# A two-layer encoder on one core: the MLP products on pairs of 2-byte floats, with range sums and the former program behind a branch

## The chip, the cores and the metric

One core of a Trainium2 chip (trn2) runs the whole forward pass as one program. The metric is the device time of one execution in microseconds (us). Engines are named as in the profile: PE multiplies matrices (PEld is its weight load), DVE, ACT and POOL work on vectors, SP issues most of the DMAs.

## The reference, cut to what matters

Two layers on a sequence of 1024 rows of width 1024. Each layer has a token mixer (latent attention in layer 0, dilated windows in layer 1) and then an MLP with a hidden width of 4096. All tensors are float32. What the change touches is the last two lines:

```python
for i in range(DEPTH):                       # 2
    ...
    x = x + gate1 * y                        # y: the token mixer
    h = rms_norm(x, norm_mlp[i]) * (1 + scale2) + shift2
    x = x + gate2 * (jnp.square(jax.nn.relu(h @ mlp_w1[i])) @ mlp_w2[i])
```

## The kernel before

**How a product is made.** PE multiplies in a reduced float32 form (`fp32r`). A float32 factor x is therefore split in two: ACT copies it to the high part (`split`, line 121, or `form`, line 375), DVE subtracts to get the low part (line 122, or line 376). A product is three matmuls, high by high, high by low and low by high (`mm3`, lines 425 to 427). In the MLPs each of them has 128x128 weights and 512 moving columns.

**Both MLPs** (`mlp7`) cut each of the two big products into 2 x 2 blocks and use seven block products where eight would be plain. The block sums that this needs are made on DVE (line 1098, the helper `tt`) before the split.

The *up* half goes over 16 chunks `c` of 256 hidden columns and seven products each: 12 matmuls per product (4 blocks of depth, 3 matmuls). For each chunk DVE makes four weight sums (`ws`), seven low parts (`wf`), seven reads of PSUM (`ua`, `u`, `ub`) and four sums of results (`us`, `ua`); ACT makes seven high parts, relu and square (lines 1139, 1140). POOL stores the seven result blocks to DRAM (`uf`). A form is written in the code four products ahead of its use.

The *down* half goes over seven products and eight groups `g`, 24 matmuls per step. A step loads a block of `uf` and a block of `mlp_w2` (`d_load`, tiles `ufr` and `w2r`), and splits both (`d_form`, tiles `dh` and `dl`). For the first of the seven products each group loads two blocks of `mlp_w2` into the pool `G` and subtracts one from the other (`w2r<-w2r,w2r`, 1024 columns); the later products reuse them.

At the start of the up half two things overlap: the last matmuls of the mixer's output projection (`psy`), and the making of seven forms of h (`h_forms`, tiles `hk`, `hs`, `ht`, `hf`), each in two tiles of 1024 columns. The first six chunks have their first weights formed early (`mlp_early`, tiles `w1h`, `wf` in the pool `G`), so that PE starts with 12 products that need only two of the seven forms of h.

**What sets the order.** The framework places each engine's instructions by a timeline of its own while it builds the program, so that a load or a vector operation stands where its buffers are expected to be free, often far from where the code calls it. Each engine then runs its queue in order. The buffers of `G` (29, also for `hf`, early `wf`, `woh`, `oT`, `w2r` of the first down product) and of `X` (20, for `w1r`, `ws`, other `wf`, `ufr`, `dh`, `dl`) are 4 KB per partition each, whatever a tile uses of it.

**The branch that is there already.** `bias_check` (line 1366 on) finds on the chip whether the positions are evenly spaced; the flag is read by every engine (line 1396) and a branch (line 1484) skips the general bias tables.

Of the kernel before, what the change touches and what calls it, by code (L numbers as in the profile page):

```python
# [20 lines left out]
P = 128  # L21
D = 1024
# [19 lines left out]
class K:  # L42
    def __init__(self, ctx, tc, a, ng=29):
        self.ctx, self.tc, self.nc, self.a = ctx, tc, tc.nc, a
        nc = tc.nc
        self.cp = ctx.enter_context(tc.tile_pool(name="const", bufs=1))
# [5 lines left out]
        self.n = 0  # L52
        self.ax = None
# [16 lines left out]
    def nm(self, s):  # L70
        self.n += 1
        return f"{s}_{self.n}"
# [10 lines left out]
    def C(self, name, shape, dt=F32):  # L83
        return self.cp.tile(list(shape), dt, tag=name, name=name)

    def M(self, name, shape, dt=F32):
        return self.mp.tile(list(shape), dt, tag=name, name=name)


    def setup(self):  # L90
# [5 lines left out]
        nc.vector.memset(self.ones, 1.0)  # L96
        self.mods = {}
        self.gates = self.dp.tile([4, 1024], F32, name="gates")
        self.onerow = self.dp.tile([1, S], F32, name="onerow")
# [19 lines left out]
    def split(self, hi, lo, src, lo_eng=None):  # L119
        nc = self.nc  # L120
        nc.scalar.activation(hi, src, AF.Copy)  # L121
        (lo_eng or nc.vector).tensor_tensor(lo, src, hi.bitcast(F32), op=ALU.subtract)  # L122
# [31 lines left out]
    def consts(self, psp):  # L154
# [6 lines left out]
        self.pinned(nc.vector.tensor_copy(self.colc, ps[:, 0:136]))  # L161

# [54 lines left out]
    def ada_col(self, l, s, c, n, ps):  # L217
# [7 lines left out]
        nc.vector.tensor_tensor(mo, ps, self.colc[:, b : b + nd], op=ALU.add)  # L225
# [9 lines left out]
    def ada_end(self, l, s, acc, row, psp, tag):  # L235
# [3 lines left out]
        if s % 3 == 2:  # L239
            for h in range(2):  # L240
                ps, c = PS(), slice(h * 512, (h + 1) * 512)
                nc.tensor.matmul(ps[0:1, :], self.ones[:, 0:1], acc[:, c], start=True, stop=True)
                nc.vector.tensor_tensor(row[0:1, c], ps[0:1, :], row[0:1, c], op=ALU.add)
# [118 lines left out]
    def h_forms(self, xs0, xs1, mods, xalloc):  # L362
# [176 lines left out]
    def mla(self, xs, ada0, xs1, mods, tail):  # L539
# [168 lines left out]
        qkv = self.dp.tile([H, S, 256], F32, name="qkv")  # L708
        hw = [w0, []]
        heads, maxes = {}, {}  # L710
        md, ld, rd = (self.dp.tile([H, S], F32, name=x) for x in ("mrow", "lrow", "rrow"))
# [126 lines left out]
        oTd = self.dp.tile([4, 2, P, 2, 512], F32, name="moTd")  # L838
# [170 lines left out]
    def proj_res(self, O, order, wo, gate, xs, mods, xalloc, done, more, first=None):  # L1009
# [4 lines left out]
        with self.tc.tile_pool(name="psO", bufs=2 if first else 6, space=PSUM, reuse_waits="tile") as psp:  # L1014
# [21 lines left out]
            pss = []  # L1036
            (at, steps), (at1, steps1) = self.h_forms(xs[0:4], xs[4:8], mods, xalloc)
# [29 lines left out]
    def w1_form(self, src, alloc):  # L1067

        g = alloc("wf", (P, 2, 4, P))
        self.split(g[:, 0], g[:, 1], src)  # L1070
        return g

    def mlp_early(self, l, E):
# [7 lines left out]
        def form(c):  # L1081
            raw = raws.pop(c)
            for g in range(2):
                Ls[c][f"L1{g + 1}"] = self.w1_form(raw[:, 4 * g : 4 * g + 4, :], self.G)
# [3 lines left out]
    def mlp7(self, l, early, R, steps, xd, out, more=(), nxt=None, keep=None):  # L1088
# [10 lines left out]
        uf = self.dp.tile([7, NP, P, 512], F32, name=f"uf{l}")  # L1099
# [5 lines left out]
        with self.tc.tile_pool(name="psM", bufs=8, space=PSUM, reuse_waits="tile") as psp:  # L1105
# [23 lines left out]
            def up(u, i):  # L1129
# [6 lines left out]
                def square(o, x, y):  # L1136
# [3 lines left out]
                    nc.scalar.activation(o, o, AF.Square)  # L1140
# [46 lines left out]
            def d_form(i, g, ld):  # L1187
# [8 lines left out]
                split(u)  # L1196
                if rn == "R11":
                    split(q["11"])
                if rn == "R11":
# [129 lines left out]
            for n, (i, gr) in enumerate(dsteps):  # L1329
# [20 lines left out]
                if n == last - 1:  # L1350
                    continue
                for t in range(4):
# [13 lines left out]
    def bias_check(self, psp):  # L1366
# [5 lines left out]
        self.bias = [self.dp.tile([9, H, self.HS], F32, name=f"bias{g}") for g in range(3)]  # L1372
# [10 lines left out]
        nc.vector.tensor_scalar(fl, ps[0:1, 0:1], 0.0, None, op0=ALU.is_equal)  # L1383

        pf = self.G("posrf", (8, P), F32)
# [5 lines left out]
        self.fl = fl  # L1391

    def bias_even_load(self):

        nc = self.nc
        loads, (self.even,) = nc.values_load_multi_w_load_instructions(
# [1024 lines left out]
```

## Time and profile before

| what | us |
|---|---|
| runs, lowest / median / highest of 3 | 3220.20 / 3229.61 / 3231.48 |
| profiled execution, first to last instruction (span) | 3228.3 |
| what lies around the span (median of the runs less the span; the profiled execution's own time is not given apart) | 1.3 |
| MLP of layer 0, first to last matmul, about | 777 to 1402 |
| MLP of layer 1, first to last matmul, about | 2602 to 3222 |
| PE busy / DVE busy / ACT busy | 3127.8 / 2381.4 / 1734.1 |

In the profile a matmul's own duration is longer than the distance to the next one, since matmuls are pipelined: what counts for the time is the distance from start to start. A row of the timeline has the start in us, the duration in us, engine, line, operation, output tile and input tiles, shapes and count. A row of the windows has, for a stretch of the span, its length and each engine's busy time with the number of instructions in brackets, then the granted clock of PE (1.00 is full speed), the DMA engines' busy share and GB/s. In the list of groups the two numbers behind the bar are busy us and mean ns of one instruction.

### The profile page before, as it was taken

How to read it: one execution, taken by the hardware profiler on the slowest of the kernel's cores; microseconds unless marked ns; L12 is line 12 of the kernel's file. 1: busy time of each engine (PE TensorE's matmuls, PEld its weight loads, DVE VectorE, ACT ScalarE, POOL GpSimd, SP SyncE). 2: the span in 40 equal slices, each digit the busy share in tenths (PEclk: the TensorE clock that was granted, in tenths of full speed). 3: DMA queues.
4: the chain of work that ended last, by engine and by line, in shares of the span. 5: the costliest groups of instructions: out<-in, count | busy, mean ns of one | idle time of the engine just before them, and what ended most of it. 6: DMA issues, size and time to landing. Idle time of an engine off the chain costs nothing. (4 is left out here: it accounts for less than half of the span.)

```text
span 3228.3 us, 50796 instructions
## 1 busy us (share of the span) xinstructions
PE 3127.8 (97%) x18034; PEld 2646.1 (82%) x18034; DVE 2381.4 (74%) x4243; ACT 1734.1 (54%) x3507; POOL 919.3 (28%) x1226
## 2 busy tenths in 40 slices
PE   6989999999999999989999999998999999999999
PEld 6877677778788788877889998998998888888887
DVE  5677777746977776688857777777887588778566
ACT  5547777754544443542226777667665264544342
POOL 6464556530111100001123435444454001110010
PEclk8999999999999999999999999999999999999999
DMA  5352322253554779555648777887777536448554
GB/s 193 121 190 79 106 87 92 67 170 111 181 200 170 270 218 315 171 194 172 213 128 185 180 174 177 185 196 169 173 159 199 171 105 214 150 151 313 202 190 130
DMA packets 540014, 554.41 MB, mean 172 GB/s; under 512 B 199493, under 2 KB 421106, under 8 KB 539754
## 3 DMA queue, kind: packets, MB, share of 16 engines
q1 hardware_dynamic: 501962, 445.10, 48.7%
q0 software_dynamic: 27360, 91.31, 7.6%
q10 hardware_dynamic: 10432, 14.68, 1.6%
q8 instruction: 144, 2.36, 0.3%
q14 instruction: 116, 0.95, 0.1%
HBM read 378.27 MB, written 132.62 MB: 158 GB/s over the span
## 5 line engine op out<-in xcount | busy, mean ns | idle before, releaser
L426 PE MATMUL psm<-dl,dh 128*128 128x512 f32 x896 | 351.1, 392 | 8.6 <-DVE dl L122 8.4
L425 PE MATMUL psm<-hf,wf 128*128 128x512 f32 x896 | 350.2, 391 | 2.6 <-ACT wf L121 2.6
L427 PE MATMUL psm<-dh,dl 128*128 128x512 f32 x896 | 350.2, 391 | 0.0
L426 PE MATMUL psm<-hf,wf 128*128 128x512 f32 x896 | 349.4, 390 | 0.0
L427 PE MATMUL psm<-hf,wf 128*128 128x512 f32 x896 | 346.9, 390 | 0.4 <-DVE wf L122 0.4
L425 PE MATMUL psm<-dh,dh 128*128 128x512 f32 x896 | 334.7, 391 | 4.7 <-ACT dh L121 4.7
L425 PE MATMUL psproj<-wqkh,hTp 128*128 128x256 f32 x1024 | 302.7, 296 | 0.0
L427 PE MATMUL psproj<-wqkh,hTp 128*128 128x256 f32 x1024 | 291.5, 285 | 0.0
L426 PE MATMUL psproj<-wqkl,hTp 128*128 128x256 f32 x1024 | 291.3, 285 | 0.0
L121 ACT ACTIVATE dh<-ufr 128x1024 fp32r<-128x1024 f32 x112 | 118.4, 1057 | 173.1 <-PE psm L427 50.1
L426 PEld LDWEIGHTS psm<-dl,dh 128*128 128x128 f32 x896 | 169.0, 189 | 46.7 <-DVE dl L122 11.8
L425 PEld LDWEIGHTS psproj<-wqkh,hTp 128*128 128x128 f32 x1024 | 197.6, 193 | 8.4 <-issue 0.2
L425 PEld LDWEIGHTS psm<-dh,dh 128*128 128x128 f32 x896 | 168.4, 188 | 41.8 <-ACT dh L121 6.8
L425 PEld LDWEIGHTS psm<-hf,wf 128*128 128x128 f32 x896 | 168.7, 188 | 40.2 <-ACT wf L121 5.5
L427 PEld LDWEIGHTS psm<-hf,wf 128*128 128x128 f32 x896 | 168.5, 188 | 36.0 <-DVE wf L122 1.2
L426 PEld LDWEIGHTS psproj<-wqkl,hTp 128*128 128x128 f32 x1024 | 197.8, 193 | 0.2 <-DVE wqkl L122 0.2
L427 PEld LDWEIGHTS psproj<-wqkh,hTp 128*128 128x128 f32 x1024 | 197.6, 193 | 0.2
L427 PEld LDWEIGHTS psm<-dh,dl 128*128 128x128 f32 x896 | 169.0, 189 | 34.8
L426 PEld LDWEIGHTS psm<-hf,wf 128*128 128x128 f32 x896 | 168.7, 188 | 34.6
L122 DVE TENSOR_TENSOR dl<-ufr,dh 128x1024 fp32r<-128x1024 f32 x112 | 136.9, 1222 | 77.8 <-ACT dh L121 59.1
L756 DVE TENSOR_REDUCE mx<-pmx 128x1 f32<-128x512 f32 x256 | 165.0, 682 | 27.6 <-PE pmx L754 27.4
L122 POOL TENSOR_TENSOR pl<-p,ph 128x1024 fp32r<-128x1024 f32 x58 | 141.3, 2435 | 136.2 <-ACT ph L121 125.9
(400 smaller groups left out, 8917.1 us busy)
## 6 DMA issues: line engine op xcount, KB each, us to landing
ufr<-uf SPq DMA_DIRECT2D x112, 512.0 KB
adaw<-in_ada_w SPq DMA_DIRECT2D x96, 512.0 KB
w2r<-in_mlp_w SPq DMA_DIRECT2D x96, 512.0 KB
w1r<-in_mlp_w SPq DMA_DIRECT2D x64, 512.0 KB
bt<-bias SPq DMA_DIRECT2D x128, 256.0 KB
wqkr<-in_dil_w_in SPq DMA_DIRECT2D x96, 256.0 KB
wvr<-in_dil_w_in SPq DMA_DIRECT2D x34, 512.0 KB
qkv<-st SPq DMA_DIRECT2D x32, 512.0 KB
```

What stands on the lines that cost most here:

```text
L121: nc.scalar.activation(hi, src, AF.Copy)
L122: (lo_eng or nc.vector).tensor_tensor(lo, src, hi.bitcast(F32), op=ALU.subtract)
L425: mm(out, lh, rh, start=first, stop=False)
L426: mm(out, lh, rl, start=False, stop=False)
L427: mm(out, ll, rh, start=False, stop=last)
L756: nc.vector.tensor_reduce(maxes[h][:, 2 * j + b : 2 * j + b + 1], ps, op=ALU.max, axis=AX.X)
```

## The change

- **2-byte pairs in the MLPs.** All operands of both MLPs' matmuls (`hf`, `wf`, and `d` for the former `dh`, `dl`) become pairs of float16 in one tile of 4 KB (`pair`), where two tiles of 4 KB or one tile of two float32 halves stood. The number of matmuls, their shapes and the three-matmul scheme stay. PE gets a separate weight load for each matmul. The mixers stay as they are.
- **Scales.** Powers of two keep the values in the range of float16: h is 16 times as large (folded into the modulation's rows), weights 512 times (in the copy and the subtraction), the square takes a scale of 2^-10, the gate 2^-15.
- **Range sums.** The low part is made by one DVE instruction that scales, subtracts and also sums the low part over the columns into a column of a tile `seen` (`parts`). Three high parts per layer are summed in absolute value (`floor`). At the end of each MLP these columns are folded to one number per partition, and at the very end of the second one a comparison and a 1x1 matmul give one flag (`verdict`, `verdict_sum`).
- **The former program behind a branch.** `program` calls `run` twice: once as described, and once more, with the float32 forms and tiles named `r_...`, inside `tc.If(k.good_value == 0)`. Every engine reads the flag and branches at its end. The bias tables are shared.

The core of the diff:

```diff
+    def pair(self, alloc, name, shape):
+        if self.half:
+            g = alloc(name, (shape[0], 2) + tuple(shape[1:]), F16)
+            return g[:, 0], g[:, 1]
+        return tuple(alloc(name + k, shape) for k in "hl")
...
+    def parts(self, hi, lo, src, scale=1.0):
+        if not self.half:
+            return self.split(hi, lo, src)
+        nc = self.nc
+        nc.scalar.activation(hi, src, AF.Copy, scale=scale)
+        self.nseen += 1
+        return nc.vector.scalar_tensor_tensor(lo, src, scale, hi, op0=ALU.mult, op1=ALU.subtract,
+                                              accum_out=self.seen[:, self.nseen - 1 : self.nseen])
...
+    def fold(self, k):
+        tr, s = self.nc.vector.tensor_reduce, self.seen
+        tr(self.bad[:, k : k + 1], s[:, 0 : self.nseen], op=ALU.add, axis=AX.X, apply_absolute_value=True)
+        tr(self.bad[:, k + 2 : k + 3], s[:, 509 : self.nlow + 1], op=ALU.min, axis=AX.X)
...
+        nc.vector.tensor_scalar(t[:, 0:2], self.bad[:, 0:2], 512.0, None, op0=ALU.is_le)
+        nc.vector.tensor_scalar(t[:, 2:4], self.bad[:, 2:4], 128.0, None, op0=ALU.is_ge)
+        nc.vector.tensor_reduce(m, t, op=ALU.min, axis=AX.X)
...
+        nc.tensor.matmul(ps[0:1, 0:1], m, self.ones[:, 0:1], start=True, stop=True)
+        self.good = self.C("good", [1, 1], I32)
+        nc.vector.tensor_scalar(self.good, ps[0:1, 0:1], float(P), None, op0=ALU.is_equal)
...
-            g = [self.G("hf", (P, 2, 512)) for _ in range(2)]
-            nc.scalar.activation(g[0], src, AF.Copy)
-            lo = nc.vector.tensor_tensor(g[1], src, g[0].bitcast(F32), op=ALU.subtract)
+            g = self.pair(self.G, "hf", (P, 2, 512))
+            lo = self.parts(*g, src)
...
-        g = alloc("wf", (P, 2, 4, P))
-        self.split(g[:, 0], g[:, 1], src)
+        g = alloc("wf", (P, 2, 4, P), F16 if self.half else F32R)
+        self.parts(g[:, 0], g[:, 1], src, self.ws)
...
-                def split(x):
-                    r.extend(self.X("d" + k, (P, 2, 512)) for k in "hl")
-                    self.split(*r[-2:], x)
+                def split(x, scale=self.ws):
+                    r.extend(self.pair(self.X, "d", (P, 2, 512)))
+                    self.parts(*r[-2:], x, scale)
...
 def program(tc, a):
+    with tc.tile_pool(name="shared", bufs=1, space=DRAM) as shared:
+        k = run(tc, a, True, shared)
+        with tc.If(k.good_value == 0):
+            run(tc, a, False, shared, k)
```

With the buffers that the pairs leave free, the framework orders some queues anew. Three places matter. First PE, at the first product of layer 0's MLP (`hf` are the forms of h, `wf` the formed weights). Before:

```order
L425 MATMUL psm_14029<-hf_13717,wf_13875 128x512
L426 MATMUL psm_14029<-hf_13718,wf_13875 128x512
L427 MATMUL psm_14029<-hf_13717,wf_13875 128x512
L425 MATMUL psm_14029<-hf_13717,wf_13875 128x512
L426 MATMUL psm_14029<-hf_13718,wf_13875 128x512
```

And now:

```order
L504 LDWEIGHTS wf_13879
L504 MATMUL psm_14034<-hf_13724,wf_13879 128x512
L505 LDWEIGHTS wf_13879
L505 MATMUL psm_14034<-hf_13724,wf_13879 128x512
L506 LDWEIGHTS wf_13879
L506 MATMUL psm_14034<-hf_13724,wf_13879 128x512
```

The weight load is an instruction of its own, and both halves of a form of h lie in one tile. The matmuls are the same.

Second SP's queue, at the start of the same MLP (`w1h` and `w1r` are raw weights of the up half, `w2r` those of the down half). Before:

```order
L431 DMA w1h_14188<-in_mlp_w 128x8x128
L431 DMA w1r_14329<-in_mlp_w 128x4x256
L431 DMA w1r_14331<-in_mlp_w 128x4x256
L431 DMA w2r_16479<-in_mlp_w 128x2x512
L431 DMA w1r_14433<-in_mlp_w 128x4x256
L431 DMA w1r_14435<-in_mlp_w 128x4x256
```

And now:

```order
L510 DMA w1h_14191<-in_mlp_w 128x8x128
L510 DMA w1r_14324<-in_mlp_w 128x4x256
L510 DMA w2r_16474<-in_mlp_w 128x2x512
L510 DMA w2r_16476<-in_mlp_w 128x2x512
L510 DMA w1r_14326<-in_mlp_w 128x4x256
L510 DMA w2r_16498<-in_mlp_w 128x2x512
L510 DMA w2r_16500<-in_mlp_w 128x2x512
L510 DMA w2r_16524<-in_mlp_w 128x2x512
L510 DMA w2r_16526<-in_mlp_w 128x2x512
L510 DMA w2r_16549<-in_mlp_w 128x2x512
L510 DMA w2r_16551<-in_mlp_w 128x2x512
```

Fourteen of the sixteen blocks of `mlp_w2` for the first down product moved from the end of the up half to its start; the next weights of the up half (`w1r_14428`) stand behind them. Before, one of the sixteen stood there. Layer 1 has the same.

Third DVE's queue, some 50 us into the same MLP (`ws` are weight sums of the up half, `ub` reads of PSUM). Before:

```order
L122 TENSOR_TENSOR wf_14373<-ws_14221,wf_14373 128x512
L1098 TENSOR_TENSOR ws_14351<-ws_14351,w1r_14200 128x512
L1098 TENSOR_TENSOR ws_14352<-w1r_14202,ws_14351 128x512
L1098 TENSOR_TENSOR ub_14409<-psm_14413,u_3042_14407 128x512
L1098 TENSOR_TENSOR ub_14409<-psm_14437,u_3042_14407 128x512
L122 TENSOR_TENSOR wf_14391<-ws_14351,wf_14391 128x512
L122 TENSOR_TENSOR wf_14410<-ws_14352,wf_14410 128x512
```

And now:

```order
L1180 TENSOR_TENSOR w2r_16476<-w2r_16476,w2r_16474 128x1024
L151 SCALAR_TENSOR_TENSOR wf_14368,seen_13378<-ws_14222,wf_14368 128x512
L1180 TENSOR_TENSOR ws_14346<-ws_14346,w1r_14201 128x512
L1180 TENSOR_TENSOR w2r_16500<-w2r_16500,w2r_16498 128x1024
L1180 TENSOR_TENSOR ws_14347<-w1r_14203,ws_14346 128x512
L1180 TENSOR_TENSOR ub_14404<-psm_14408,u_3029_14402 128x512
L1180 TENSOR_TENSOR ub_14404<-psm_14432,u_3029_14402 128x512
L151 SCALAR_TENSOR_TENSOR wf_14386,seen_13378<-ws_14346,wf_14386 128x512
L1180 TENSOR_TENSOR w2r_16526<-w2r_16526,w2r_16524 128x1024
L151 SCALAR_TENSOR_TENSOR wf_14405,seen_13378<-ws_14347,wf_14405 128x512
```

Seven of the eight subtractions of `w2r` now stand between the up half's forms; before, all eight stood at the end of the up half. The eighth is still there.

More of the change, by code (lines that the diff above doesn't have):

```diff
@@ L1371, in bias_check @@
         self.HS = P * 257
-        self.bias = [self.dp.tile([9, H, self.HS], F32, name=f"bias{g}") for g in range(3)]
+        if not self.half:
+            return self.positions(psp)
+        self.bias = [self.shared.tile([9, H, self.HS], F32, name=f"bias{g}") for g in range(3)]
         d, df = self.G("cdiff", (73, 16), I32), self.G("cdifff", (73, 16), F32)
@@ L2294, in program @@
             k.reload(O, src, pp, 1)
-        xm = [k.dp.tile([S, D], F32, name=f"xm{l}") for l in range(2)]
+        xm = [k.DR([S, D], f"xm{l}") for l in range(2)]
         keep_x = lambda l: (lambda t: nc.gpsimd.dma_start(out=xm[l][t * P : (t + 1) * P, :], in_=xs[t]))
```

128 lines of the change are left out of this document (97 added, 31 removed).

## The prediction

> **What bounds the kernel now.** I read the page first: the engines' busy time and the chain of work that ended last.
>
> ```profile
> PE 3127.8 (97%) x18034; PEld 2646.1 (82%) x18034; DVE 2381.4 (74%) x4243; ACT 1734.1 (54%) x3507; POOL 919.3 (28%) x1226
> PE 21%; DMA 1%; DVE 1%; issue 0%; ACT 0%; DVEq 0%; ACTq 0%; SPq 0%
> ```
>
> PE is the bound on the average and nearly alone in the chain. The average hides stages, so the windows come next, three per MLP: start of the up half, rest of it, down half. Columns: PE, PEld, DVE, ACT, POOL, then clock, DMA share, GB/s.
>
> ```profile
> 777.00:860.00 83.00, 81.84 (x374) 66.73 (x373) 69.91 (x100) 50.73 (x82) 6.05 (x10) 1.00 0.41 136
> 860.00:1089.00 229.00, 229.00 (x1007) 188.17 (x1006) 179.82 (x281) 112.79 (x191) 35.46 (x52) 1.00 0.56 195
> 1089.00:1399.00 310.00, 297.56 (x1325) 243.57 (x1325) 219.03 (x243) 132.03 (x143) 9.23 (x16) 0.98 0.77 243
> 2601.00:2690.00 89.00, 87.16 (x394) 72.02 (x393) 77.40 (x115) 53.58 (x88) 9.10 (x13) 0.98 0.44 144
> 2690.00:2912.00 222.00, 222.00 (x981) 183.90 (x980) 160.42 (x257) 109.96 (x185) 32.76 (x48) 1.00 0.47 169
> 2912.00:3222.00 310.00, 307.96 (x1351) 252.53 (x1350) 216.61 (x219) 115.83 (x116) 15.31 (x28) 1.00 0.61 206
> ```
>
> In the middle of both up halves PE never idles. DVE is busy for 79% and 72% of these stretches, and 84% and 87% at the starts. A timeline of PE gives the true cost of a matmul, and the groups give their number.
>
> ```profile
> 999.74 0.39 PE L427 MATMUL psm<-hf,wf 128*128 128x512 f32 x1
> ...
> 1003.82 0.39 PE L427 MATMUL psm<-hf,wf 128*128 128x512 f32 x1
> L425 PE MATMUL psm<-hf,wf 128*128 128x512 f32 x896 | 350.2, 391 | 2.6 <-ACT wf L121 2.6
> L425 PEld LDWEIGHTS psm<-hf,wf 128*128 128x128 f32 x896 | 168.7, 188 | 40.2 <-ACT wf L121 5.5
> ```
>
> The two starts are 18 steps apart: 4.08/18 = 0.2267 us per matmul of 512 columns. Six such groups of 896 (three lines, two halves) make 5376 matmuls, so 1218.7 us of the span. The rest of the MLPs' time is small waits of PE:
>
> ```profile
> 1093.33 0.50 PE L426 MATMUL psm<-dl,dh 128*128 128x512 f32 x1 [2.54 <-DVE dl L122]
> 1376.27 1.19 PE L425 MATMUL psm<-dh,dh 128*128 128x512 f32 x4 [3.24 <-ACT dh L121]
> 1381.59 0.80 PE L426 MATMUL psm<-dl,dh 128*128 128x512 f32 x1 [4.13 <-DVE dl L122]
> 1360.00:1380.00 20.00, 13.06 (x67) 9.82 (x65) 20.00 (x29) 13.75 (x18) 1.08 (x2) 0.94 0.54 197
> 1380.00:1400.00 20.00, 18.36 (x72) 14.41 (x73) 17.62 (x20) 7.18 (x8) 1.08 (x2) 0.89 0.63 204
> ```
>
> After such a wait the granted clock falls (0.89 in the last row), so a wait costs more than its length. In the row above it DVE is busy for all of 20 us, and PE for 13.
>
> **The change, part by part. The matmul itself.** The nearest rows with 2-byte operands are the mixer's `psav` products (bf16 moving, float16 weights, own weight loads):
>
> ```profile
> 1711.91 0.26 PE L1989 MATMUL psav<-vs,pT 128*128 128x192 bf16 x1
> 1712.00 0.22 PE L1990 MATMUL psav<-vs,pT 128*128 128x128 bf16 x1
> ...
> 1712.89 0.25 PE L1989 MATMUL psav<-vs,pT 128*128 128x192 bf16 x1
> L1990 PEld LDWEIGHTS <-pT 128*128 128x128 f16 x640 | 63.7, 100 | 0.4 <-issue 0.3
> ```
>
> Seven pairs of 192+128 columns take 0.98 us, 0.140 per 320 columns. If the fp32r row and this one have the same time per column, 2.4 columns per ns (an estimate: 512 in 213.3 and 13.4 over; 320 in 133.3 and 6.7 over, 3.3 per matmul), a float16 matmul repeats every 216.7 ns: 10.0 ns saved, x5376 = **53.8 us**. The ends: the overhead grows with the columns (0.140 x 512/320 = 224 ns), which saves 2.7 ns or 14.5 us; or no overhead remains beyond 2 ns, about 61 us. I take a fixed overhead, because it comes once per instruction in both rows. The weight loads stay hidden: in these rows they take 100 ns and matmuls follow every 70 ns all the same; in the MLP there are 217 ns to hide them.
>
> **DVE's new instruction.** The low part changes from a subtraction to a scaled one with a sum. The rows:
>
> ```profile
> L122 DVE TENSOR_TENSOR wf<-ws,wf 128x512 fp32r<-128x512 f32 x128 | 85.8, 687 | 0.5 <-ACT wf L121 0.5
> L122 DVE TENSOR_TENSOR dl<-ufr,dh 128x1024 fp32r<-128x1024 f32 x112 | 136.9, 1222 | 77.8 <-ACT dh L121 59.1 <-issue 17.3
> L176 DVE SCALAR_TENSOR_TENSOR adacc<-adaw,cond,adacc x84: 1270/1285/2889, 17.7 to 2991.5; 128x1024 f32<-128x1024 f32 x84
> L1932 DVE DVE_READ_ACCUMULATOR2_ANT stat<- 128x1 f32 x384 | 31.7, 82 | 0.0
> L1938 ACT ACTIVATION_READ_ACCUMULATOR pd<-pd,dnb 128x1 f32 x384 | 71.8, 187 | 0.0
> L1976 DVE TENSOR_TENSOR ph<-pd,ph x65: 673/694/1598, 1688.5 to 2243.4; 128x512 f16<-128x512 f32 x65
> ```
>
> The three-operand form costs 1285 - 1222 = 63 ns more; reading the sum, if it is an instruction of its own, about 82 (DVE's row; ACT's says 187). A 2-byte output costs nothing (694 against 687). So +0.145 us per split, between 0.06 and 0.31; about 238 splits per layer make +35 us of DVE. Seven of them stand in each up-half chunk of 84 matmuls, which takes 84 x 0.2267 = 19.05 us now and 18.2 after. By the middle windows DVE works 15.0 us of a chunk in layer 0 (179.82/229) and 13.8 in layer 1 (160.42/222); +1.0 makes 16.0 and 14.8, or 88% and 81% of 18.2: covered by PE's own time, so nothing there. That cover ends at 18.2 us of DVE per chunk.
>
> **The starts of the up halves** have less cover. There DVE runs almost without a gap, and the chain passes through it:
>
> ```profile
> 791.82 0.69 DVE L1098 TENSOR_TENSOR ua<-psm,ua 128x512 f32<-128x512 f32 x1 [2.38 <-PE psm L427]
> ...
> 830.62 0.68 DVE L1098 TENSOR_TENSOR ua<-psm,u 128x512 f32<-128x512 f32 x1
> 833.12 0.69 DVE L1098 TENSOR_TENSOR u<-psm,ua 128x512 f32<-128x512 f32 x1 [1.81 <-PE psm L427]
> 2633.27 0.50 PE L425 MATMUL psm<-hf,wf 128*128 128x512 f32 x1 [1.84 <-ACT wf L121]
> L1098 DVE TENSOR_TENSOR w2r<-w2r,w2r 128x1024 f32<-128x1024 f32 x16 | 19.4, 1223 | 10.4 <-DMA w2r<-in_mlp_w 10.4
> ```
>
> About 31 splits stand in these 40 us: +4.5 us. PE reaches the same place about 2.4 us earlier (some 180 matmuls at 0.0133 x 10.0/13.4). Three to seven of the moved `w2r` subtractions can fall in too (1.22 us each); the queue puts them between the forms, and the next `wf` waits behind each. As part of this lands in slack, I take **+8 us** of waits per layer, with the slow clock after them, 2 to 15: **+16** in all. The same subtractions leave the end of the up half, where DVE had room.
>
> **The moved loads.** SP issues fourteen 512 KB blocks before the next `w1r`. Their place has an idle DMA before:
>
> ```profile
> GB/s 193 121 190 79 106 87 92 67 170 111 181 200 170 270 218 315 171 194 172 213 128 185 180 174 177 185 196 169 173 159 199 171 105 214 150 151 313 202 190 130
> 800.00:820.00 20.00, 19.24 (x83) 14.99 (x82) 18.87 (x24) 14.43 (x21) 0.00 (x0) 1.00 0.05 13
> 829.48 1.62 SPq L431 DMA_DIRECT2D w1r<-in_mlp_w  x2
> ```
>
> 14 x 0.52 MB take 23 us at 315 GB/s, the highest slice of the page, so the `w1r` behind them lands near 843 instead of soon after 829. By the order of the queue it belongs to the chunk after next, 19 to 30 us on. I take 0, at worst a wait of 5.
>
> **The down halves.** A step's forms take half the buffers of `X`, so loads and splits can run further ahead; the first product's `w2r` is there already. The windows show what can go: 1325 matmuls x 0.2267 = 300.4 of 310 us in layer 0, 306.3 of 310 in layer 1, some 13 us. I credit **10**, between 0 and 20 (with the starts' own waits). Each step's DVE work becomes 0.3 us longer in 5.2 us of PE; DVE's 219 us of 310 leave room.
>
> **Start, folds and the end.** Two small POOL operations and two rows of scales at the start cost nothing: they have no reader for hundreds of us. The folds and the flag come before the last product is done. The last branch is on every engine's path, SP's too. The kernel has one such branch already:
>
> ```profile
> L1396 SPq TENSOR_LOAD <-dfl x1: 475/475/475, 11.8 to 11.8; - x1
> L1484 PEldq COMPARE_BRANCH  x1: 6310/6310/6310, 5.3 to 5.3; - x1
> 3223.67 1.87 SPq L2372 DMA_DIRECT2D out<-x  x3
> ```
>
> PE's queue was held for 6.3 us. SP issues its last output at 3225.5, and the data land by 3228.3; with 0.5 of reading and 6.3 of branch SP ends at 3232.3. That is **+4**, between 0.6 (the branch not taken costs nothing) and 7. [...]
>
> **The sum.** 3228.3 - 53.8 + 16 - 10 + 4 = 3184.5, and 1.3 for what lies around the span: **3186 us**. The profiled span lies 1.3 under the median of the runs, so the sum can be held against the median 3229.6 as it is. I take 0.5% (16 us) for about what a measurement of this kernel can tell from no change: faster below 3213.5, slower above 3245.8.
>
> **The rivals.** (a) DVE becomes the bound. If a split costs 0.31 more, a chunk in layer 0 needs 15.0 + 2.2 = 17.2 of 18.2 us, and each start gets 31 x 0.31 = 9.6 us plus seven subtractions of 1.22, 18 us together, less nothing for slack, and 4 per layer more in the down half. 3229.6 - 53.8 + 44 + 4 = 3224: no change. For it: DVE is busy for all of 1360 to 1380, and the waits there name it. Against: both accumulator rows lie near 0.1 to 0.2.
> (b) The overhead grows with the columns: 3229.6 - 14.5 + 6 + 4 - 5 = 3220, no change. Against it stands that one instruction, not one column, is what both rows share.
> (c) Weight loads no longer hide. A separate load that must wait for the matmul ahead of it costs its 100 ns: 213 + 100 = 313 in place of 226.7, x5376 = +464, so 3694: slower. It decides once more than 10 ns of a load show per matmul. Against it: `psav` runs loads of 100 ns at 70 ns a matmul. [...]
> (d) The range test sends the kernel into the old program: 2 x 3200 = about 6400. The low parts are rounding errors of either sign, about 0.005 each where values lie near 16 (11 bits); 512 or 1024 of them sum to 0.1 to 0.2, and 240 such sums to 24 to 48, ten times under the limit of 512.
> [...]
>
> **How the numbers follow.** Forecast 0.80, (a) 0.09, (b) 0.06, (c) 0.03, (d) 0.01, (e) 0.01. The forecast's own bounds: the best, 61 saved, 20 credited, 4 lost at the starts and 0.6 at the end, gives 3153; the worst, 30 at the starts, 0 credited, 7 at the end, gives 3213. All ends rarely meet, so its likely part is 3164 to 3205; (a) and (b) reach above, and the range goes to 3214. Faster: the forecast, a third of (a) and (b), and (e), 0.86; no change: the rest of (a) and (b), 0.10; slower 0.04.
>
> **What would show it.** In the new profile: `psm` matmuls 0.217 apart; loads of 100 ns beside them; splits of 0.75 to 0.85 (512) and 1.37 (1024), or a separate accumulator row; PE waits in the first 50 us of each MLP that name `wf`, `hf` or `ws`; fewer waits for `dl` in the down halves; a branch of some 6 us at the end on SP. A pitch of 224 or over 226 makes the main term wrong; DVE at 95% or more through the up halves makes (a) right.

## The result, and the profile after

| what | before | after |
|---|---|---|
| median of the runs, us | 3227.06 | 3172.76 |
| lowest to highest of 4 | 3220.20 to 3231.48 | 3169.30 to 3175.89 |
| span of the profiled execution | 3228.3 | 3174.0 |

After over before is 0.9832, 95% interval 0.9816 to 0.9847: 1.7% faster, some 54 us. Forecast were 3186 us and 3164 to 3214.

The page of the profile after, engines first, then the chain that ended last:

```profile
PE 3072.2 (97%) x18036; PEld 2165.6 (68%) x18036; DVE 2385.7 (75%) x4734; ACT 1726.4 (54%) x3507; POOL 918.5 (29%) x1228
PE 20%; DVE 2%; issue 0%; DMA 0%; ACT 0%; DVEq 0%
```

PE is still the bound, and DVE has grown by 4 us in all, not by 70: 491 more DVE instructions cost little busy time. The windows by stage (for layer 0 the start, middle and down half; for layer 1 the same; columns as before):

```profile
812.00:860.00 48.00, 42.95 (x184) 17.57 (x185) 46.54 (x86) 27.47 (x44) 3.45 (x5) 0.96 0.70 247
860.00:1085.00 225.00, 225.00 (x1039) 101.34 (x1038) 192.27 (x389) 115.23 (x199) 37.51 (x55) 1.00 0.60 212
1085.00:1391.00 306.00, 301.09 (x1425) 140.10 (x1422) 224.97 (x363) 138.41 (x155) 9.22 (x16) 0.99 0.74 236
2602.00:2650.00 48.00, 43.75 (x193) 18.95 (x194) 47.41 (x88) 26.23 (x42) 3.48 (x5) 0.96 0.76 270
2650.00:2872.00 222.00, 222.00 (x1031) 100.64 (x1029) 176.99 (x371) 115.39 (x197) 37.49 (x55) 1.00 0.51 183
2872.00:3165.00 293.00, 293.00 (x1354) 131.73 (x1352) 208.70 (x328) 113.62 (x116) 15.31 (x28) 1.00 0.60 198
```

The middles are full as before. In the 48 us at the starts DVE is at 97% and 99%, and PE at 89% and 91%: there the gain leaks away. Before, in the same stretch of layer 0, DVE was at 94% and PE at 99%; the prediction's 84% is the mean of a longer stretch, with room in its first part.

```profile
812.00:860.00 48.00, 47.60 (x210) 38.91 (x209) 45.09 (x69) 27.26 (x45) 5.52 (x9) 1.00 0.50 170
```

Down halves are nearly full. A timeline of PE in the middle of layer 0's up half:

```profile
984.76 0.38 PE L504 MATMUL psm<-hf,wf 128*128 128x512 f16 x1
...
989.94 0.38 PE L504 MATMUL psm<-hf,wf 128*128 128x512 f16 x1
```

24 steps in 5.18 us: 0.2158 us per matmul, 10.9 ns less than the 0.2267 of before. 5376 of them are **58.6 us**.

What a stage loses is now read exactly. From the starts of all 2688 matmuls of one MLP I take away their number times the pitch (0.2267 before, 0.2158 after); what is left is waits, the slow clock after them (0.96 in the two starts above, 1.00 in the middles), and PE's other work. Excess in us by the number of the matmul (1344 is the turn to the down half):

| | start, 0 to 336 | middle, to 1344 | turn, to 1440 | rest | sum |
|---|---|---|---|---|---|
| before, layer 0 | 5.9 | 2.0 | 4.4 | 22.0 | 34.4 |
| after, layer 0 | 12.0 | 1.9 | 0.0 | 14.6 | 28.5 |
| before, layer 1 | 7.4 | 0.0 | 2.0 | 2.4 | 11.8 |
| after, layer 1 | 10.6 | 0.0 | 0.0 | 2.4 | 13.0 |

The account of the two spans: -58.6 by the pitch; +9.3 at the two starts; -13.8 in the down halves and turns; the first matmul of the first MLP at 782.4 in place of 777.1, +5.3; the second mixer 1.3 longer; the end 2.4 longer (9.2 from the last product's start to the end of the span, 6.9 before). The sum, -54.1, is the difference of the spans, -54.3, but for rounding.

The 5.3 us ahead of the first MLP lie in a part of the program that the change leaves nearly as it is. About half of them come at one place, shown by the windows from the same wait on, before and then after:

```profile
225.00:232.00 7.00, 6.79 (x37) 6.18 (x38) 3.47 (x11) 2.63 (x9) 4.21 (x14) 1.00 0.35 115
```

```profile
227.00:237.00 10.00, 9.48 (x38) 8.82 (x38) 3.92 (x11) 2.97 (x10) 4.19 (x14) 0.69 0.51 158
```

The same 37 or 38 matmuls, but the granted clock is 0.69 in place of 1.00. In the eleven traces of the changed kernel and its variants, all with the same work of the mixer ahead of it, the first MLP starts anywhere from 777.9 to 782.5, and the second mixer takes 1176.7 to 1183.5 us (1179.8 before). So most of this is scatter from one execution to the next. The 777.1 of the one trace of before lies under all eleven, whose median is 779.4, so that up to some 2 us of it may belong to the change; this stays open.

### The profile page after: what moved, and what is told of

Its sections match the earlier page's. It is cut to its first block, busy times and chain, and to the rows that moved or that the text cites. A ratio compares the mean times of both kernels' runs of the same rounds, so it can differ in the third digit from the quotient of the medians.

```text
span 3174.0 us, 51216 instructions
## 1 busy us (share of the span) xinstructions
PE 3072.2 (97%) x18036; PEld 2165.6 (68%) x18036; DVE 2385.7 (75%) x4734; ACT 1726.4 (54%) x3507; POOL 918.5 (29%) x1228
## 3 DMA queue, kind: packets, MB, share of 16 engines
q8 instruction: 146, 2.39, 0.3%
## 5 line engine op out<-in xcount | busy, mean ns | idle before, releaser
L504 PE MATMUL psm<-hf,wf 128*128 128x512 f16 x896 | 340.8, 380 | 5.1 <-ACT wf L148 5.1
L505 PE MATMUL psm<-d,d 128*128 128x512 f16 x896 | 340.4, 380 | 4.7 <-DVE d L151 4.7
L505 PE MATMUL psm<-hf,wf 128*128 128x512 f16 x896 | 341.1, 381 | 0.0
L506 PE MATMUL psm<-d,d 128*128 128x512 f16 x896 | 340.3, 380 | 0.0
L506 PE MATMUL psm<-hf,wf 128*128 128x512 f16 x896 | 335.4, 381 | 4.7 <-DVE wf L151 4.6
L504 PE MATMUL psm<-d,d 128*128 128x512 f16 x896 | 334.7, 380 | 0.3 <-ACT d L148 0.3
L148 ACT ACTIVATE d<-ufr 128x1024 f16<-128x1024 f32 x112 | 117.8, 1052 | 206.2 <-PE psm L506 172.2
L151 DVE SCALAR_TENSOR_TENSOR d<-ufr,d 128x1024 f16<-128x1024 f32 x112 | 136.7, 1220 | 80.7 <-ACT d L148 80.5
L947 ACT ACTIVATE p<-pss 128x512 f32<-128x512 f32 x256 | 144.5, 589 | 51.7 <-PE pss L934 50.6
L1979 POOL TENSOR_TENSOR qn<-qn,dgain 128x256 f32<-128x256 f32 x96 | 89.8, 935 | 285.2 <-DVE qn L1977 238.3
L2035 ACT ACTIVATE pd<-pd,dnb 128x192 f32<-128x192 f32 (+2 forms) x384 | 167.7, 438 | 3.7 <-ACT dnb L2033 2.1
L2088 DVE TENSOR_REDUCE U<-psav 128x128 f32<-128x384 f32 x192 | 103.1, 551 | 86.4 <-PE psav L2087 86.1
L506 PEld LDWEIGHTS <-wf 128*128 128x128 f16 x896 | 88.0, 98 | 114.4 <-DVE wf L151 9.0
L504 PEld LDWEIGHTS <-wf 128*128 128x128 f16 x896 | 87.9, 98 | 113.6 <-ACT wf L148 9.6
```

What stands on the lines that cost most here:

```text
L148: nc.scalar.activation(hi, src, AF.Copy, scale=scale)
L151: return nc.vector.scalar_tensor_tensor(lo, src, scale, hi, op0=ALU.mult, op1=ALU.subtract, accum_out=self.seen[:, self.nseen - 1 : self.n ...
L504: mm(out, lh, rh, start=first, stop=False)
L505: mm(out, lh, rl, start=False, stop=False)
L506: mm(out, ll, rh, start=False, stop=last)
L947: nc.scalar.activation(p[:, b * 512 : (b + 1) * 512], ps[b], AF.Exp)
```

## The experiments

All times are medians; "the changed kernel" is 3172.8 us, 0.9832 of before. It did not run again beside the variants; the medians of before beside them lie between 3227.9 and 3228.7 (3227.1 beside the changed kernel), so differences of 1 or 2 us between medians tell nothing, and the traces are what decides. The tables of excess are made as above from each run's own trace, with the pitch 0.2158.

**1. No branch.**

```diff
-        with tc.If(k.good_value == 0):
-            run(tc, a, False, shared, k)
...
-            k.good_value = k.flag_load(k.good)
```

> The new program without the branch at its end and without the former program behind it; the flag is still worked out but nobody reads it. In the profile of the changed kernel SP's branch begins at 3169.1 and SP goes on at 3171.8, and the span ends 9.2 us after the last product of the MLP, where it was 6.9 before the change. Theory A (the branch costs what SP's own row shows, about 2.3 to 3 us, and nothing anywhere else): 2 to 4 us faster than the changed kernel, so about 3169 to 3171 (ratio to before 0.982). Theory B (twice the code makes the whole program slower through its fetching of instructions, for example the 5.3 us by which the first MLP starts later): 6 to 10 us faster, about 3164. Theory A has the end of the span 6.5 to 7 us after the last product, and the first MLP's start anywhere between 777 and 783.

Measured: 3167.2 us, ratio 0.9808 (0.9792 to 0.9824). The first MLP starts at 782.5, both MLPs have the excess of the changed kernel (29.1 and 13.0), and the end takes 5.7 us in place of 9.2: the branch costs some **3.5 us** there, and the trace shows nothing of it anywhere else. The other variants, which all have the branch, take 8.7 to 10.2 for the end where one program runs, so this is known to about 1 us. The end is shorter than the 6.5 to 7 that theory A had, and the gain of 5.5 us between the medians lies between the two theories; but theory B's place for it, an earlier first MLP, is not there. Theory A stands. SP's and PE's rows of the branch in the changed kernel:

```profile
L2356 SPq EVENT_SEMAPHORE  x8: 17/17/17, 3171.8 to 3172.3; - x8
L2356 PEldq COMPARE_BRANCH  x1: 4157/4157/4157, 3161.6 to 3161.6; - x1
L2356 SPq COMPARE_BRANCH  x1: 58/58/58, 3169.1 to 3169.1; - x1
```

The branch itself takes 58 ns on SP, but SP's next instruction comes 2.7 us later.

**2. No sums.** The splits don't sum, the sums of absolute values are left out, and constants stand in `seen`: the range test is left out.

```diff
-        return nc.vector.scalar_tensor_tensor(lo, src, scale, hi, op0=ALU.mult, op1=ALU.subtract,
-                                              accum_out=self.seen[:, self.nseen - 1 : self.nseen])
+        return nc.vector.scalar_tensor_tensor(lo, src, scale, hi, op0=ALU.mult, op1=ALU.subtract)
...
```

> The splits keep their scaled subtraction but sum nothing, and the three sums of absolute values per layer are left out; the columns of the flag are filled with constants, so the range test is left out. Theory A (the reading of the sum, 0.083 us, lies beside the next DVE instruction: splits follow each other 0.61 us apart with it as without it): no change against the changed kernel, within 2 us, and the starts of the up halves keep 10 to 12 us of waits each. Theory B (the prediction's term, 0.145 us per split, on the path at the starts): 8 to 16 us faster, the waits at the starts halved.

Measured: 3179.0 us, ratio 0.9838 (0.9821 to 0.9856): no gain. By the medians it is 6.2 us slower than the changed kernel, where theory A had no change within 2. Starts 12.1 and 10.3, against 12.0 and 10.6: theory A there. The first MLP loses 5.3 us more between matmuls 1440 and 2352, where PE waits once for a sum of the modulation, no part of what was left out, and the granted clock is lower behind it (0.77 in this stretch, 1.00 in the changed kernel):

```profile
1243.13 3.07 PE L325 MATMUL psac<-ones,adacc 128*128 128x1 f32 x16 [1.76 <-DVE adacc L246]
1240.00:1255.00 15.00, 13.24 (x55) 6.96 (x54) 10.61 (x11) 8.33 (x9) 0.00 (x0) 0.77 0.93 329
```

Why the sums are nearly free is seen in DVE's timeline of the changed kernel:

```profile
986.28 0.68 DVE L151 SCALAR_TENSOR_TENSOR wf<-w1r,wf 128x512 f16<-128x512 f32 x1
986.89 0.08 DVE L151 DVE_READ_ACCUMULATOR wf<-w1r,wf 128x1 f32 x1
986.89 0.69 DVE L1180 TENSOR_TENSOR ua<-psm,ua 128x512 f32<-128x512 f32 x1
987.50 0.68 DVE L151 SCALAR_TENSOR_TENSOR wf<-ws,wf 128x512 f16<-128x512 f32 x1
```

The read of the sum and the next instruction start together, at 986.89. From split to next instruction it is 0.61 us. Over all splits of 512 columns that have the next instruction right behind them, the median distance is 0.611 us here, 0.602 in the run without sums and 0.601 before the change; with 1024 columns it is 1.145, 1.135 and 1.135. So a sum costs some 0.01 us, and 476 of them about make the 4 us by which DVE has grown. The third operand costs nothing:

```profile
L151 DVE SCALAR_TENSOR_TENSOR d<-ufr,d 128x1024 f16<-128x1024 f32 x112 | 136.7, 1220 | 80.7 <-ACT d L148 80.5
```

1220 ns, where the plain subtraction took 1222.

**3. Two buffers per form of h.** So the first down product's weights find no buffer early, and all their subtractions are back around the end of the up half (1068 to 1102 us in layer 0).

```diff
+        if self.half and name == "hf":
+            return tuple(alloc(name + k, shape, F16) for k in "hl")
         if self.half:
             g = alloc(name, (shape[0], 2) + tuple(shape[1:]), F16)
```

> The forms of h take two buffers again, as before the change, so that the weights of the first down product are loaded, and all eight of their subtractions made, at the end of the up half as before; all else is as in the changed kernel. Theory A (the seven moved subtractions, 1.14 us each on a DVE that has no room there, make the 9 us by which the starts of the two up halves are worse than before): waits in the first 336 products of each up half fall from 12.0 and 10.4 us to 6 to 8, and the kernel is 4 to 8 us faster at the starts; the turn to the down half gives back 2 to 4 in each layer (it waited 4.0 and 2.0 there before the change and 0 after). Together 0 to 5 us faster than the changed kernel. Theory B (PE reaches the same DVE work earlier, whoever stands in DVE's queue): starts as in the changed kernel, and 4 to 6 us slower by the turns.

Measured: 3177.5 us, ratio 0.9842 (0.9825 to 0.9858). Starts 7.4 and 8.2: theory A there, the moved subtractions cost the starts 4.6 and 2.4 us, 7.0 of the 9.3. PE's waits from 800 to 880 in the changed kernel, and from 796 to 880 here:

```profile
PE psm L506 <- DVE wf L151: 2.5, 4, 1.1
PE psm L504 <- ACT wf L148: 2.4, 4, 1.3
```

```profile
PE psm L506 <- ACT wf L150: 2.4, 3, 0.9
PE psm L508 <- DVE wf L153: 0.5, 1, 0.5
```

But the turns go from 0 to 7.2 and 5.0 us, more than the 2 to 4 expected. The wait there names the split:

```profile
PE psm L507 <- DVE d L153: 4.5, 2, 4.0
```

So against this run the move more than pays for itself: 7.0 lost at the starts, 12.2 won at the turns and 1.2 further on, some 6 us on balance, near the 4.7 between the medians. The expectation had 0 to 5 us the other way, by turns of 2 to 4. Against the turns as they were before the change (4.4 and 2.0) the move would about pay for itself and no more; why this run's turns are longer than those was not tried.

**4. The subtractions on POOL.**

```diff
-                    tt(q["12"], q["12"], q["11"], ALU.subtract)
+                    nc.gpsimd.tensor_tensor(q["12"], q["12"], q["11"], op=ALU.subtract)
```

> The subtractions of the first down product's weights go from DVE to POOL, which is busy for under a tenth of the starts; loads and buffers stay as in the changed kernel. On POOL such an operation takes about 2.4 us in this kernel's profile. Theory A (they are what DVE lacks at the starts): waits in the first 336 products fall from 12.0 and 10.4 to 6 to 8 us, the turns stay at 0: 6 to 10 us faster than the changed kernel, about 3164. Theory B (PE's earlier arrival alone): no change within 2 us. A third way: POOL's operation makes DVE's instructions beside it longer, seen as DVE rows over 0.69 and 1.23 us at 830 to 850, and the gain is lost.

Measured: 3188.1 us, ratio 0.9872 (0.9855 to 0.9888): about 15 us slower than the changed kernel. Starts 18.5 and 17.1, all else as there. It is the third way, and worse than that. POOL and DVE of this run:

```profile
825.64 2.33 POOL L1284 TENSOR_TENSOR w2r<-w2r,w2r 128x1024 f32<-128x1024 f32 x1 [44.47 <-DMA w2r<-in_mlp_w]
829.81 5.52 POOL L1284 TENSOR_TENSOR w2r<-w2r,w2r 128x1024 f32<-128x1024 f32 x2 [1.83 <-DMA w2r<-in_mlp_w]
837.06 6.97 POOL L1284 TENSOR_TENSOR w2r<-w2r,w2r 128x1024 f32<-128x1024 f32 x3
```

```profile
825.67 2.85 DVE L151 SCALAR_TENSOR_TENSOR wf<-w1r,wf 128x512 f16<-128x512 f32 x1
830.38 2.72 DVE L1180 TENSOR_TENSOR ws<-w1r,ws 128x512 f32<-128x512 f32 x1
833.03 1.27 DVE L1180 TENSOR_TENSOR ub<-psm,u 128x512 f32<-128x512 f32 x2
838.94 0.69 DVE L1180 TENSOR_TENSOR u<-psm,ua 128x512 f32<-128x512 f32 x1 [1.22 <-PE psm L506]
839.61 4.98 DVE L151 SCALAR_TENSOR_TENSOR wf<-w1r,wf 128x512 f16<-128x512 f32 x1
```

A split of 0.68 us takes 2.85 or 4.98: it ends about half a us after POOL is done (844.59 against 844.03). DVE instructions with an operand in PSUM run beside the same POOL operations at their usual time: two `ub` in 1.27 us from 833.03, a `u` in 0.69 from 838.94.

**5. Two buffers per form of the down half.**

```diff
+        if self.half and name == "d":
+            return tuple(alloc(name + k, shape, F16) for k in "hl")
         if self.half:
             g = alloc(name, (shape[0], 2) + tuple(shape[1:]), F16)
```

> Each form of the down halves takes two buffers of X again, as before the change, high and low part apart; all else is as in the changed kernel, the weights of the first product early too. Theory A (half the buffers let loads and splits run further ahead, and that took most of the waits of the later down half: 6.4 to 4.1 and 15.4 to 10.4 us in layer 0): waits behind the first 96 products of the down half come back, 3 to 8 us in layer 0, and the kernel is 3 to 9 us slower than the changed one. Theory B (the turns' gain, 4.4 and 1.6 us, comes from the early weights and the rest is a matter of the clock): no change within 2 us in the down halves.

Measured: 3182.5 us, ratio 0.9862 (0.9845 to 0.9878), 9.7 slower than the changed kernel, of which the trace shows 7 in layer 0's MLP. There the last 336 matmuls lose 16.8 us (10.4 in the changed kernel, 15.6 before), 1440 to 2352 lose 4.8 (4.2); layer 1 is as in the changed kernel (2.2). Theory A in layer 0. The two waits that it brings stand where two stood before the change, one of which (the first) the changed kernel has not:

```profile
1353.57 1.02 PE L506 MATMUL psm<-dh,dh 128*128 128x512 f16 x4 [2.77 <-ACT dh L150]
1358.91 0.58 PE L507 MATMUL psm<-dl,dh 128*128 128x512 f16 x1 [4.31 <-DVE dl L153]
```

```profile
1369.46 0.38 PE L505 MATMUL psm<-d,d 128*128 128x512 f16 x1 [4.65 <-DVE d L151]
```

The second fence is the changed kernel: one wait for DVE remains, and is no shorter.

**6. One more DVE instruction per split.**

```diff
+        nc.vector.tensor_reduce(self.sm("more", 1), self.ident[:, 0:3], op=ALU.add, axis=AX.X)
```

> One more DVE instruction behind each split, a sum of three columns, which took 0.15 us where the changed kernel has such a row; its result is not used. It puts back on DVE what the prediction expected each split to cost, about 0.145 us. Theory A (the start of the up half is bound by DVE, so that what stands there shows in full): the waits in the first 336 products rise by 31 to 40 times 0.15, 4.5 to 6 us, in each layer, to about 16 us each, nothing in the middle, 0 to 3 in the down halves: 10 to 14 us slower than the changed kernel, about 3185. Theory B (the starts wait for something else, a load or the clock): under 3 us per start.

Measured: 3181.6 us, ratio 0.9859 (0.9843 to 0.9875), 8.8 slower. Starts 15.7 and 14.3, that is 3.7 and 3.7 more; middle and down halves as they were, but for 0.6.

But the run is not the one that the expectation describes. The new instruction reads only `ident`, and the framework placed all 476 of them at the two starts (736 to 864 and 2540 to 2670 us), in groups between the other work and not one behind each split:

```profile
L153 DVE TENSOR_REDUCE more<-ident x476: 143/159/196, 736.3 to 2670.2; 128x1 f32<-128x3 f32 x159
800.69 0.47 DVE L153 TENSOR_REDUCE more<-ident 128x1 f32<-128x3 f32 x6
801.07 0.69 DVE L1182 TENSOR_TENSOR ws<-w1r,w1r 128x512 f32<-128x512 f32 x1
```

Six of them take 0.38 us, 0.063 each, though a row lasts 0.159. Behind the first matmul of an MLP stand some 230, all of them in its first 100 us: some 14.4 us of DVE, of which 3.7 show in PE's time. The windows of the first 78 us, in the changed kernel and then here, say where the rest went:

```profile
782.00:860.00 78.00, 72.94 (x339) 33.00 (x338) 66.63 (x119) 46.10 (x73) 3.98 (x6) 0.98 0.56 192
```

```profile
779.00:857.00 78.00, 70.79 (x327) 32.26 (x325) 75.36 (x321) 42.28 (x67) 3.28 (x5) 0.96 0.55 183
```

DVE had 11.4 us free there, 9.9 of them in the first 30 us, and has 2.6 left. So theory A has the place right, since work added to DVE at the start delays PE; that it "shows in full" is wrong here, since DVE's gaps take most of it. What 0.15 us behind each split would cost was not measured. With this run's instructions the two starts together lose 16.7 us more than before the change; that this is near the +16 of the prediction is chance.

**7. Four matmuls of 128 columns for one of 512, in the up halves.**

```diff
-                for d in range(4):
-                    rh, rl = (r[k][d // 2][:, d % 2, :] for k in range(2))
-                    self.mm3(ps, w[:, 0, d, :], w[:, 1, d, :], rh, rl, d == 0, d == 3)
+                for e in range(0, 512, 128):
+                    for d in range(4):
+                        rh, rl = (r[k][d // 2][:, d % 2, e : e + 128] for k in range(2))
+                        self.mm3(ps[:, e : e + 128], w[:, 0, d, :], w[:, 1, d, :], rh, rl, d == 0, d == 3)
```

> In the up halves each matmul of 512 columns is made as four of 128, each with its own weight load: 2688 become 10752; the down halves stay. Theory A (a float16 matmul costs its columns at 2.4 per ns and about 2.5 ns, once per instruction, and a load of 98 ns is hidden however short the matmul): a matmul of 128 columns every 56 ns, four in 223 to 227 instead of 215.8: 20 to 30 us slower than the changed kernel, about 3195 to 3200. Theory B (the overhead grows with the columns): four in 216, no change. Theory C (loads show once they are longer than the matmul): one every 98 ns, 392 for four: 470 us slower, about 3640.

Measured: 3201.4 us, ratio 0.9921 (0.9905 to 0.9938), 28.6 slower: theory A. PE's timeline:

```profile
989.80 0.22 PE L506 MATMUL psm<-hf,wf 128*128 128x128 f16 x1
...
991.98 0.22 PE L506 MATMUL psm<-hf,wf 128*128 128x128 f16 x1
900.00:1080.00 180.00, 180.00 (x3198) 178.34 (x3196) 144.55 (x295) 88.33 (x153) 28.59 (x42) 1.00 0.53 180
```

39 steps in 2.18 us: 55.9 ns per 128 columns, and 215.8 per 512. The 384 columns between them take 159.9 ns, 2.4 columns per ns, and some 2.5 ns per instruction are left over in both. Loads fill PEld to 99%, one of 98 ns for each of these, and still none shows in a pitch of 55.9 ns.

```profile
L505 PEld LDWEIGHTS <-wf 128*128 128x128 f16 x3584 | 351.2, 98 | 0.0
```

Of the 28.6 us the pitch makes 21.0 (2688 times 4 x 55.9 - 215.8). The rest is no matter of the matmul: by the trace the two turns lose 14.2 us here, where the changed kernel loses none (PE waits 5.4 for a split in layer 0), and the starts 5.3 less.

**8. The early weights in the middle of the up half.** Seven pairs are loaded and subtracted one by one (`w2_early`, not shown), from product 44 on, every eight products, at a fixed place of the queues.

```diff
...
+            for g in range(7 if self.half else 0):
+                put(44 + 8 * g, w2_early, g)
...
```

> Seven of the eight pairs of weights of the first down product are loaded and subtracted in the middle of the up half, one pair per chunk of the later chunks, neither at its start (as in the changed kernel) nor at its end (as before). DVE has room there: PE waits for nothing between products 336 and 1344. Theory A (the moved subtractions cost the starts 2 to 5 us each, and the early loads save the turns 7 and 3): the starts as with two buffers per form of h, 7.4 and 8.2 us, the turns as in the changed kernel, 0: 6 to 8 us faster than the changed kernel, about 3166. Theory B (the middle has no such room, DVE at 85% there being too full for 1.2 us more per chunk): 2 us or more of new waits in the middle of each layer, no gain.

Measured: 3177.9 us, ratio 0.9846 (0.983 to 0.9863): no gain. Layer 1 does what theory A has: start 7.1, nothing in the middle, nothing at the turn, 9.5 in all against 13.0. Layer 0 does what theory B has: start 9.7, but 5.8 in the middle, where waits of 0.2 to 0.8 us for `wf` appear, and 6.2 at the turn. DVE shows the cause of the last:

```profile
1085.31 1.28 DVE L247 SCALAR_TENSOR_TENSOR adacc<-adaw,cond,adacc 128x1024 f32<-128x1024 f32 x1 [7.25 <-DMA adaw<-in_ada_w]
1087.71 1.22 DVE L151 SCALAR_TENSOR_TENSOR d<-ufr,d 128x1024 f16<-128x1024 f32 x1
```

A sum of the modulation, which only layer 0 does there, waits 7.25 us for its data, and the split of the first down product stands behind it on DVE. Its load was issued late, behind the eighth pair of the weights and three blocks of `uf`:

```profile
1067.93 1.67 SPq L510 DMA_DIRECT2D w2r<-in_mlp_w  x2
1069.70 1.46 SPq L510 DMA_DIRECT2D ufr<-uf  x3
1071.21 0.81 SPq L340 DMA_DIRECT2D adaw<-in_ada_w  x1
```

In the changed kernel two such loads stand ahead of that pair, from 1046.89 on. The framework moved the second; that the pairs at fixed places are why is likely, and was not tried.

**9. The same in layer 1 alone.**

```diff
-            for g in range(7 if self.half else 0):
+            for g in range(7 if self.half and l == 1 else 0):
...
```

> The early weights of the first down product in the middle of the up half as in the run before, but in layer 1 alone; layer 0 is the changed kernel's. Theory A (each layer's waits are its own): layer 0's MLP as in the changed kernel (28 us of waits in all, 608 us long), layer 1's as in the run before (9.5 of waits, 589.4): 3.5 us faster than the changed kernel's 3172.8, about 3169, which is within what the measurement can tell; the table of waits shows it. Theory B (layer 1's better start was a matter of the run): layer 1's waits 13 again.

Measured: 3171.2 us, ratio 0.9821 (0.9807 to 0.9834). Layer 0 has 28.4 of excess, layer 1 9.5, as expected. By its trace it is the best version that keeps every part, ahead of the changed kernel by the 3.5 us of layer 1; the medians, 1.5 apart, don't prove it.

**10. The test fails.** The limit is -1, so the former program runs behind the new one, and the output is its.

```diff
-        nc.vector.tensor_scalar(t[:, 0:2], self.bad[:, 0:2], 512.0, None, op0=ALU.is_le)
+        nc.vector.tensor_scalar(t[:, 0:2], self.bad[:, 0:2], -1.0, None, op0=ALU.is_le)
```

> The limit of the range test is set to -1, so that the test fails and the former program runs behind the new one; both are computed, and the output is the former program's. It shows what the prediction's rival (d) would have cost, and that the branch was not taken in the other runs. Both theories: the new program's 3165, a taken branch of some 4 to 8 us on each engine, and the former program's 3228: 6395 to 6410 us.

Measured: 6390.8 us in one run, 4 under the range expected. That is about the price of rival (d), and the other runs did not pay it.

## Why the prediction was right, point by point

**The whole.** The main term and its mechanism are right, and it is most of the result. The other terms were less sure than their sum looks: the span was forecast at 3184.5 and measured at 3174.0. The matmuls, the starts, the down halves and the end came out faster than forecast by 4.8, 6.7, 3.8 and 1.6 us, all on one side; 6.6 us in the mixers, which the sum left out, took part of it back.

**The matmul.** The mechanism and nearly the size: 10.0 ns were forecast, 10.9 measured, so 58.6 us for 53.8. The overhead per instruction is 2.5 ns, not the 3.3 that the short run of `psav` pairs, timed to 0.01 us, gave. That it comes once per instruction was a choice in the prediction; run 7 shows it. The 2.4 columns per ns of the estimate are measured too: by run 7 (384 columns in 159.9 ns), and before by `psproj`, whose 256 columns repeat every 119.5 ns (20 steps in 2.39 us from 1700.99) where 512 take 226.7, so 256 more in 107.2. Rivals (b) and (c) fall with run 7. For (e), 0.01 among the chances and counted there as faster, no run shows a basis; the pitch measured is 215.8 ns.

**DVE's new instruction: the term that failed.** The prediction had "+0.145 us per split, between 0.06 and 0.31". Measured: some 0.01, below the range. 63 ns were taken from `adacc`'s row, which is also a three-operand form, but with other operands; here the form takes as long as the subtraction. 82 ns is what the reading takes, as forecast, but not what it costs, since the next instruction starts beside it. The duration of a row was taken for its distance to the next.

**The starts.** Forecast +16 in all, measured +9.3. The reasoning about the place holds: PE waits there for `wf`, from DVE or from ACT, and ACT in turn waits, among others, for DVE's `ws` (6.9 us in four waits from 800 to 880); work added to DVE there delays PE (run 6 adds some, run 4 stretches it, run 3 takes some away). The size was wrong by the split's price, and partly saved by luck. Of the terms added up for one layer, the splits' 4.5 us were nearly nothing (31 x 0.01); the 2.4 for PE's earlier arrival is 1.8 by its own numbers (180 x 0.0133 x 10.0/13.4); with three to seven subtractions that leaves 5.5 to 10.3, and 6.1 and 3.2 were measured. The step down to 8 for slack, which was not worked out, hid most of the wrong price. Of the 9.3, the moved subtractions make 7.0 (run 3); the other 2.3, PE's earlier arrival by the likeliest reading, were not tried by themselves.

**The moved loads.** Forecast 0. PE names no load at the starts; DVE waits twice for `w2r`, 1.09 and 0.30 us, within the 9.3.

**The down halves.** Forecast -10, measured -13.8. The credit was given for forms that run further ahead, and for the weights that are there already. Both are shown: with two buffers the last part of layer 0 gives 6.4 back (run 5), without the early weights the turns give 12.2 back (run 3). The second is twice the 6.4 that stood there before the change. The prediction saw that move mostly as a cost; it is a gain of about 6 against run 3, and about even against the turns as they were.

That 10 came near 13.8 is luck in part, for the room was misread. The 1325 instructions in the window of layer 0 are not all matmuls of 512 columns. Those of `psm` alone are 1252 (PE and PEld first, then only the engines that read or write `psm`):

```profile
1089.00:1399.00 310.00, 290.34 (x1252) 235.78 (x1252) 17.31 (x26) 2.38 (x4) 0.98 0.77 243
```

1252 x 0.2267 is 283.8 of 310, so 26.2 us were not pitch in layer 0, and not 9.6; a part of them is PE's small matmuls. The half also goes on to a last start at 1420.6, not to the 1402 of the table of before.

**The end.** Forecast +4, measured 2.4 between the spans and 3.5 by run 1. SP's gap is 2.7 us and not the 6.3 that PE's row at the first branch suggested; SP's own gap at that branch was 5.3 (branch at 12.4, next instruction at 17.7), and PE's at this one is 4.2. The lower bound of 0.6 doesn't follow from that sum: with 0.5 of reading and a branch that costs nothing SP ends at 3226.0, ahead of the data at 3228.3, and the term is nothing.

**Rival (a)** was near: DVE is at 97% and 99% in the starts. It stays there, since a split costs next to nothing more, and the middle of layer 0 holds 85% (192.27 of 225). **What the sum left out** is 5.3 and 1.3 us in the mixers, for the most part scatter; the medians differ by the same 54 us as the two spans, so that no larger gain is claimed.

## What to carry to other kernels

Take the price of an instruction from the distance between starts in a busy stretch, not from its duration, and from rows with the same operands: both halves of the split's wrong price were of this kind. When an instruction is put in as a test, look in the trace where it went before reading a price off the result: in run 6 the framework put all of them elsewhere. When a change frees buffers, look at what the framework puts into them: work that moves to where its engine is full costs there, and what it saves lies elsewhere, so count both ends. Before moving work to an idle engine, look in a trace at what its instructions do to the other engine's beside them: in run 4 a split of 0.68 us took 2.85 and 4.98.

## What the runs showed of the hardware that was not expected

- The reading of a DVE sum (0.083 us) runs beside the next DVE instruction: from split to next it is 0.611 us with a sum and 0.602 without (512 columns).
- A DVE sum of three columns lasts 0.159 us and takes 0.063 of DVE's time: six in 0.38 us.
- A weight load of 98 ns stays hidden under matmuls that follow every 55.9 ns.
- Beside POOL subtractions of two SBUF tiles, DVE instructions with two SBUF inputs took longer: splits 2.85 and 4.98 us for 0.68, a `ws` 2.72 for 0.69. With one of the inputs in PSUM they did not (0.69).
- The branch at the end, past the former program, takes 0.06 us on SP, and SP's next instruction comes 2.7 us later.
